# Attention of a two-layer decoder: its order worked out at build time, and small operations moved to GpSimd

## The chip, the cores and the metric

The kernel runs on one core of a Trainium2 chip. The metric is the device time of one execution in microseconds (us), here the median of three runs. A profiled execution gives a trace beside it: the time of every instruction, what each engine waited for, and TensorE's granted clock.

## The reference, cut to what matters

Two layers over 1024 positions of width 1024, all in float32. Layer A (a Mamba-2 scan) and the embedding steps aren't touched by the change. Layer B is stick-breaking attention with 16 heads of 64:

```python
kv = rmsnorm(h) @ w_kv                 # k normed per head, v
qg = rmsnorm(h) @ w_in                 # q normed per head, gate
for blk in range(8):                   # 128 queries at a time
    z = q[blk] @ k[:kend].T
    log_keep = where(strict, log_sigmoid(-z), 0)
    suffix = reverse_cumsum(log_keep) - log_keep
    weights = where(strict, exp(log_sigmoid(z) + suffix), 0)
    o[blk] = weights @ v[:kend]
out = (o * silu(gate)) @ w_out
```

Time runs backwards in the kernel, so that the suffix sums become running products of `sigmoid(-z)`, and the weights their differences. The kernel puts the difference on the values instead: `V` holds differences of neighbouring rows of v.

## The kernel before

Every float32 product is made of three matmuls: an operand is split into a high part and a low part (`hi`, `lo`), and hi x hi, hi x lo and lo x hi are summed (`split3`, `split3_some`, `terms`). The scores and the weights' products use two.

`attention` works through 8 pairs of heads (`hp`), and in each through four steps `p` = 3, 2, 1, 0 of 256 queries; 32 steps `i` in all. A step has these stages, which run in different steps at a time:

- `project` (two blocks `b` of 128 positions) and, twice a pair, `gate`: q, k, v and the gate from the weights `W[kk]` of the pair, 24 matmuls each. ScalarE copies the results to `kq` and `vr`.
- `values`: three loads on SP's queue shift `vr` by one row into `vs` (`nc.sync.dma_start(vs[0:P - 1], vr[1:P])` is the large one), two more spread its first row into `v0`; GpSimd subtracts and splits the result into `V`.
- `norm`: ScalarE squares `kq`, VectorE sums, takes the root (`Ctx.rstd`, `Ctx.rsqrt`: three small operations, then three turns of three) and multiplies `kq`.
- `flip`: TensorE transposes the normed keys and queries, ScalarE and VectorE split them into `kst`, `qh`, `ql`.
- `scores`: TensorE makes `z`, ScalarE the sigmoid into `pt`, VectorE the running product by one scan. Columns: 1024 - 128 b.
- `turn`, `product`, `fold`: TensorE transposes `pt`, ScalarE and VectorE split it into `wh` and `wl`, TensorE multiplies by `V` into `oqs`, the halves are added and gated into `GT`.

The weights of the next pair come by `Pairs.load`, one of four loads of 512 KB a step, split by `Ctx.hilo`: ScalarE makes the high part with the gain, VectorE the low part (line 110). They lie in a ring of 10 tiles and one of 2.

TensorE's order is written by hand: `step(i)` interleaves the projections of step i with the flip and scores of step i - 1 and the combination of step i - 2, at the fractions in `SPREAD` and `FLIP`. The other engines' orders are the scheduler's. After the last pair `b2.fill` runs part of the output projection for two blocks (7 and 6) ahead, from `s_out`, and `b2.pw.load` loads the last stage's gate weights inside the block with the hand-made order.

Of the kernel before, what the change touches and what calls it, by code (L numbers as in the profile page):

```python
# [18 lines left out]
P = 128  # L19
# [40 lines left out]
def terms(a, b):  # L60
    return [(a[0], b[0]), (a[0], b[1]), (a[1], b[0])]

# [723 lines left out]
def attention(k, A, rawp, hT, oTd, dbg, b2, pairs):  # L786
# [6 lines left out]
    with ExitStack() as ctx:  # L793
# [18 lines left out]
        def begin_pair(st):  # L812
            st["V"], st["vr"], st["v0"] = {}, {}, {}
            st["GT"] = pairs.gt.tile([P, S], F32, name="GT")

        def project(st, b):
            W = st["W"]
            ps = mm.tile([P, 512], F32, name="mm")
            prs = []
            sl = slice(b % 4 * P, b % 4 * P + P)  # L820
            for kk in range(KT):
                whi, wlo = W[kk]
                prs += terms((hh[b // 4][:, kk, sl], hl[b // 4][:, kk, sl]), (whi[:, :384], wlo[:, :384]))
            yield from split3_some(nc, ps[:, :384], prs, 2)
            p = b // 2
            if b % 2:
                st["kq"] = wk.tile([P, 2, 2, P], F32, name="kq", bufs=2)
                st["vr"][p] = wk.tile([P, 2, P], F32, name="vr", bufs=3)
            nc.scalar.copy(st["kq"][:, b % 2], ps.rearrange("p (m c) -> p m c", c=256)[:, :, 0:128])
            nc.scalar.copy(st["vr"][p][:, b % 2], ps[:, 128:256])  # L830
            yield

        def gate(st, half):
            W = st["W"]
            gp = mm.tile([P, 512], F32, name="mm")
            sl = slice(half * 512, half * 512 + 512)
            prs = []
            for kk in range(KT):
                whi, wlo = W[kk]
                prs += terms((whi[:, 384:], wlo[:, 384:]), (hh[half][:, kk], hl[half][:, kk]))  # L840
            yield from split3_some(nc, gp, prs, 2)
            sg = wk.tile([P, 512], F32, name="sg", bufs=1)
            nc.scalar.activation(sg, gp, AF.Sigmoid)
            nc.vector.tensor_tensor(st["GT"][:, sl], gp, sg, op=ALU.mult)
            yield

        def values(st, p):

            vr = st["vr"][p]
            vs = wk.tile([P, 2, P], F32, name="vs", bufs=1)  # L850
            nc.sync.dma_start(vs[0:P - 1], vr[1:P])
            nc.sync.dma_start(vs[P - 1:P, 0], vr[0:1, 1])
            nc.sync.dma_start(vs[P - 1:P, 1], st["vr"][p + 1][0:1, 0] if p < 3 else zrow)
            st["v0"][p] = sm.tile([P, 2], F32, name="v0", bufs=4)
            for i in range(2):
                nc.sync.dma_start(st["v0"][p][:, i:i + 1], vr[0:1, i])
            nc.gpsimd.tensor_tensor(vs, vs, vr, op=ALU.subtract)  # L857
            V = st["V"][p] = wk.tile([P, 2, 256], F32R, name="V", bufs=6)
            Vx = V.rearrange("p b (x c) -> p b x c", c=64)
            d = vs.rearrange("p b (h c) -> p b h c", c=64)  # L860
            for i in range(2):
                nc.gpsimd.tensor_copy(Vx[:, i, 0::3], d[:, i])
                nc.gpsimd.tensor_tensor(Vx[:, i, 1:3], d[:, i], Vx[:, i, 0::3].bitcast(F32), op=ALU.subtract)

        def norm(st, p):
            kq = st.pop("kq")
            sq = wk.tile([P, 512], F32, name="sg", bufs=1)
            nc.scalar.activation(sq, kq.rearrange("p b m c -> p (b m c)"), AF.Square)
            n = 8
            ss = sm.tile([P, n], F32, name="kss")  # L870
            nc.vector.reduce_sum(ss, sq.rearrange("p (g d) -> p g d", d=64), axis=AX.X)
            y = k.rstd(sm, ss, n, 64, EPS, "kr")
            x = kq.rearrange("p b m (h d) -> p (b m h) d", d=64)
            nc.vector.tensor_tensor(x, x, y.unsqueeze(2).broadcast_to([P, n, 64]), op=ALU.mult)
            st["kn", p] = kq

        def flip(st, p):
            kn = st.pop(("kn", p))
            tsl = slice(p * 256, (p + 1) * 256)
            kt, qt = (trp.tile([P, 512], F32, name="tr")[:, :256] for _ in range(2))  # L880
            for m, t in ((0, kt), (1, qt)):
                for i in range(2):
                    nc.tensor.transpose(t[:, i * P:(i + 1) * P], kn[:, i, m], ident)
            qh = wk.tile([P, 2, 256], F32R, name="qh", bufs=1)
            for h in range(2):
                o = own[h]
                nc.scalar.activation(kst[o, h, tsl], kt[o], AF.Copy, scale=k.gkq[o])
            for h in range(2):
                o, x = own[h], own[1 - h]
                nc.vector.scalar_tensor_tensor(  # L890
                    kst[x, h, tsl], kt[o], k.gkq[o], kst[o, h, tsl].bitcast(F32), op0=ALU.mult, op1=ALU.subtract)
            for h in range(2):
                o, x = own[h], own[1 - h]
                nc.scalar.copy(qh[o, h], qt[o])  # L894
                nc.scalar.copy(qh[x, h], qt[o])  # L895
            for h in range(2):
                o = own[h]
                nc.vector.tensor_tensor(ql[o, h], qt[o], qh[o, h].bitcast(F32), op=ALU.subtract)
            st["q", p] = qh

        def scores(st, h, b):

            N = (NT - b) * P
            qs = slice((b % 2) * P, (b % 2) * P + P)
            parts = [(0, N)] if N <= 512 else [(0, N // 2), (N // 2, N // 2)]
            def part(i):
                qh = st["q", b // 2]
                if i == 0:
                    st["a", h, b] = wk.tile([P, S], F32, name="pt", bufs=5)
                pt = st["a", h, b]  # L910
                ko, n = parts[i]
                z = zp.tile([P, 512], F32, name="z")
                rk = kst[:, h, b * P + ko:b * P + ko + n]
                nc.tensor.matmul(z[:, :n], lhsT=qh[:, h, qs], rhs=rk, start=True, stop=False)  # L914
                nc.tensor.matmul(z[:, :n], lhsT=ql[:, h, qs], rhs=rk, start=False, stop=True)  # L915
                nc.scalar.activation(pt[:, ko:ko + n], z[:, :n], AF.Sigmoid, scale=-1.0)  # L916
                if i == len(parts) - 1:
                    nc.vector.tensor_tensor_scan(pt[:, :N], pt[:, :N], keep[:, :N], 1.0, op0=ALU.mult, op1=ALU.max)  # L918
            return [lambda i=i: part(i) for i in range(len(parts))]

        def turn(st, p, h, j0):

            lo = 2 * p
            al, ah = st["a", h, lo], st["a", h, lo + 1]
            tq = trp.tile([P, 512], F32, name="tr")
            c = 0
            blocks = []
            for j in (j0, j0 + 1):
                i0 = (j - lo) * P
                nc.tensor.transpose(tq[:, c:c + P], al[:, i0:i0 + P], ident)  # L930
                w = P
                if j > lo:
                    nc.tensor.transpose(tq[:, c + P:c + 2 * P], ah[:, i0 - P:i0], ident)  # L933
                    w = 2 * P
                blocks.append((j, c, w))
                c += w
            wh = wk.tile([P, 512], F32R, name="wh", bufs=3)
            wl = wk.tile([P, 512], F32R, name="wl", bufs=3)
            nc.scalar.copy(wh[:, :c], tq[:, :c])  # L939
            nc.vector.tensor_tensor(wl[:, :c], tq[:, :c], wh[:, :c].bitcast(F32), op=ALU.subtract)  # L940
            blocks.sort(key=lambda x: -x[2])
            st["w", h, j0] = [(j, x[:, c:c + w], w) for x in (wh, wl) for j, c, w in blocks]

        def product(st, p, h, j0):
            out = oqs[:, h * 256:h * 256 + 256]
            ws = st.pop(("w", h, j0))
            for i, (j, rhs, w) in enumerate(ws):
                nc.tensor.matmul(out[:, :w], lhsT=st["V"][j // 2][:, j % 2, h * P:(h + 1) * P], rhs=rhs,  # L948
                                 start=(j0 == 2 * p and i == 0), stop=(j0 == NT - 2 and i == len(ws) - 1),
                                 skip_group_check=True)  # L950

        def fold(st, p, h):

            hp, GT, oq = st["hp"], st["GT"], oqs[:, h * 256:h * 256 + 256]
            if h == 0:
                st["of"] = wk.tile([P, 256], F32, name="of", bufs=2)
# [4 lines left out]
            if h == 0:  # L961
                return
# [328 lines left out]
```

## Time and profile before

| | us |
|---|---|
| median of 3 runs (1846.22 to 1849.69) | 1849.6 |
| the profiled execution's own time | 1852.96 |
| its span, first to last instruction | 1851.2 |
| TensorE busy in the span | 1731.0 |
| VectorE, ScalarE, GpSimd busy | 1173.9, 903.0, 413.2 |

Busy times are shares of one span and don't add up. A busy matmul is drawn from its start to its modelled end, and matmuls overlap, so the distance between starts says what one costs. The idle time before an instruction is put down to what released it last.

### The profile page before, as it was taken

The numbers are of one execution on the slowest core, as the hardware profiler recorded it, in microseconds if no ns is written. First come the engines' busy times: TensorE is split into PE (matmuls) and PEld (weight loads), VectorE is DVE, ScalarE is ACT, GpSimd is POOL, SyncE is SP. The second block draws the span as 40 slices with busy tenths as digits, with TensorE's granted clock in tenths as the row PEclk, the third lists the DMA queues.
The fourth block names the chain that finished last, engine by engine and source line by source line (L and its number), as shares of the span: only waits on it lengthen the run. The fifth ranks groups of instructions, "written<-read, shape, count | busy, mean of one in ns | idle before, by whom it ended". The sixth has DMA issues, their size and how long they took to land.

```text
span 1851.2 us, 25501 instructions
## 1 busy us (share of the span) xinstructions
PE 1731.0 (94%) x9170; PEld 1465.7 (79%) x9170; DVE 1173.9 (63%) x2396; ACT 903.0 (49%) x1976; POOL 413.2 (22%) x452
## 2 busy tenths in 40 slices
PE   7999999999999999999998989898989998689999
PEld 6777877877877887888887878787878888577887
DVE  6687277278179554335667786868787687674332
ACT  6567358349338332124546464655555555552211
POOL 0234534524634122200000111101101113211110
PEclk9999999999999999999998999999999999899999
DMA  4222223223213743322301010101011002224110
GB/s 154 66 81 92 80 66 91 95 58 93 90 62 98 248 158 124 123 94 78 106 19 62 20 53 19 52 31 39 32 46 57 19 29 73 73 86 127 43 44 34
DMA packets 96398, 139.43 MB, mean 75 GB/s; under 512 B 18160, under 2 KB 66640, under 8 KB 96272
## 3 DMA queue, kind: packets, MB, share of 16 engines
q1 hardware_dynamic: 96272, 137.80, 23.0%
q8 instruction: 72, 1.18, 0.3%
q14 instruction: 54, 0.44, 0.1%
HBM read 108.77 MB, written 24.77 MB: 72 GB/s over the span
## 4 chain that ended last, share of the span: by engine, by line
PE 74%; DVE 14%; ACT 7%; DMA 2%; issue 2%; POOL 1%; SPq 0%; DVEq 0%; POOLq 0%; ACTq 0%
PE mm L48 36%; PE mm L55 14%; PE mm L1122 5%; PE oq L948 3%; PE pq L48 2%; DVE pt L918 2%; PE z L915 2%; DVE v L236 2%; PE intra L411 2%; PE z L914 1%; PE tr L930 1%; PE inter L406 1%; ACT qh L895 1%; PE tr L666 1%; ACT qh L894 1%
## 5 line engine op out<-in xcount | busy, mean ns | idle before, releaser
L48 PE MATMUL mm<-ul,wh 128*128 128x512 f32 (+1 forms) x648 | 254.0, 392 | 0.0
L48 PE MATMUL mm<-uh,wl 128*128 128x512 f32 (+1 forms) x648 | 252.5, 390 | 0.0
L48 PE MATMUL mm<-uh,wh 128*128 128x512 f32 (+1 forms) x648 | 252.4, 389 | 0.1
L918 DVE TENSOR_TENSOR_SCAN pt<-pt,keep 128x128 f32<-128x128 f32 (+7 forms) x128 | 174.0, 1364 | 21.9 <-ACT pt L916 20.6
L55 PE MATMUL mm<-g0h,hl 128*128 128x384 f32 x512 | 182.5, 356 | 0.0
L55 PE MATMUL mm<-g0l,hh 128*128 128x384 f32 x512 | 182.3, 356 | 0.0
L55 PE MATMUL mm<-g0h,hh 128*128 128x384 f32 x512 | 181.1, 354 | 0.0
L236 DVE SCALAR_TENSOR_TENSOR v<-u,convh,v 128x512 f32<-128x512 f32 x144 | 130.2, 909 | 55.1 <-ACT v L234 52.7
L939 ACT CAST wh<-tr 128x512 fp32r<-128x512 f32 (+1 forms) x160 | 85.4, 543 | 146.6 <-PE tr L933 141.7
L857 POOL TENSOR_TENSOR vs<-vs,vr 128x256 f32<-128x256 f32 x32 | 24.1, 754 | 567.4 <-DMA vs<-vr 489.9
L940 DVE TENSOR_TENSOR wl<-tr,wh 128x512 fp32r<-128x512 f32 (+1 forms) x160 | 100.7, 633 | 72.6 <-ACT wh L939 71.8
L48 PEld LDWEIGHTS mm<-ul,wh 128*128 128x128 f32 x648 | 121.7, 188 | 26.4 <-issue 2.3
L48 PEld LDWEIGHTS mm<-uh,wl 128*128 128x128 f32 x648 | 121.8, 188 | 25.6 <-issue 1.9
L48 PEld LDWEIGHTS mm<-uh,wh 128*128 128x128 f32 x648 | 121.7, 188 | 25.6 <-issue 1.3
L108 POOL TENSOR_TENSOR wl<-raw,wh 128x1024 fp32r<-128x1024 f32 x39 | 95.2, 2441 | 156.7 <-ACT wh L106 156.7
L916 ACT ACTIVATE pt<-z 128x320 f32<-128x320 f32 (+3 forms) x192 | 93.8, 489 | 70.0 <-PE z L915 68.1
L55 PEld LDWEIGHTS mm<-g0l,hh 128*128 128x128 f32 x512 | 99.7, 195 | 2.1
L576 DVE SCALAR_TENSOR_TENSOR acc<-mm,rg,acc 128x512 f32<-128x512 f32 x64 | 47.8, 749 | 84.2 <-PE mm L48 83.3
L55 PEld LDWEIGHTS mm<-g0h,hl 128*128 128x128 f32 x512 | 99.7, 195 | 1.6
L55 PEld LDWEIGHTS mm<-g0h,hh 128*128 128x128 f32 x512 | 99.8, 195 | 1.2
L649 DVE SCALAR_TENSOR_TENSOR pth<-pth,pq 128x512 f32<-128x512 f32 (+1 forms) x33 | 22.2, 671 | 104.9 <-PE pq L48 100.2
L373 ACT ACTIVATE ex<-ex,acum 128x128 f32<-128x128 f32 x256 | 86.5, 389 | 0.8
(368 smaller groups left out, 4334.2 us busy)
## 6 DMA issues: line engine op xcount, KB each, us to landing
raw<-in_w_in SPq DMA_DIRECT2D x40, 512.0 KB
ex<-acd SPq DMA_DIRECT2D x64, 256.0 KB
raw<-in_w_b SPq DMA_DIRECT2D x32, 512.0 KB
raw<-in_m_out SPq DMA_DIRECT2D x16, 512.0 KB
raw<-in_gate SPq DMA_DIRECT2D x16, 512.0 KB
graw<-gT SPq DMA_DIRECT2D x30, 256.0 KB
gT<-zs SPq DMA_DIRECT2D x28, 256.0 KB
acc<-in_x SPq DMA_DIRECT2D x8, 512.0 KB
```

The lines of the kernel that those rows point to most:

```text
L48: nc.tensor.matmul(out, lhsT=a, rhs=b, start=(i == 0), stop=(i == n - 1))
L55: nc.tensor.matmul(out, lhsT=a, rhs=b, start=(i == 0), stop=(i == n - 1))
L108: (eng or nc.gpsimd).tensor_tensor(lo, raw, hi.bitcast(F32), op=ALU.subtract)
L236: nc.vector.scalar_tensor_tensor(vv, u[:, 3 - j:3 - j + 512], w(j), vv, op0=ALU.mult, op1=ALU.add)
L373: nc.scalar.activation(x, x, AF.Relu, bias=acum[:, c:c + 1])
L576: nc.vector.scalar_tensor_tensor(acc[:, sl], ps, k.rg[:, g, t:t + 1], acc[:, sl], op0=ALU.mult, op1=ALU.add)
L916: nc.scalar.activation(pt[:, ko:ko + n], z[:, :n], AF.Sigmoid, scale=-1.0)
L918: nc.vector.tensor_tensor_scan(pt[:, :N], pt[:, :N], keep[:, :N], 1.0, op0=ALU.mult, op1=ALU.max)
L939: nc.scalar.copy(wh[:, :c], tq[:, :c])
L940: nc.vector.tensor_tensor(wl[:, :c], tq[:, :c], wh[:, :c].bitcast(F32), op=ALU.subtract)
L948: nc.tensor.matmul(out[:, :w], lhsT=st["V"][j // 2][:, j % 2, h * P:(h + 1) * P], rhs=rhs, start=(j0 == 2 * p and i == 0), stop=(j0 == NT ...
L1122: nc.tensor.matmul(pss[n], lhsT=a, rhs=b, start=(q == 0 and i == 0), stop=(q == 1 and i == 11))
```

## The change

The attention is no longer emitted step by step. Each operation is entered into a `Plan` with its engine, a duration, a rank, what it comes after, and the buffers that it takes and gives back; `Plan.order` lists them, always taking the operation that can start first, at equal times the one with the lower rank. They are emitted in this order, and the order is now fixed on TensorE, ScalarE, VectorE and GpSimd (before: on TensorE alone). SP's loads are planned as three engines of their own (`SPV`, `SPW`, `SPS`).

The root's three turns go to GpSimd, as four operations each. The weights' gain is applied in place by ScalarE, which then copies the high part; the low part is a subtraction on GpSimd. Scans of over 512 columns are done in two parts. Sigmoid and product of the gate are made in `GT` itself. `b2.pw.load` stands behind the block. The core of the diff:

```diff
+class Plan:
+    LAT = 0.3
...
+    def order(self):
...
+            for i in open_:
+                eng, us, rank, _, after, takes, _ = self.ops[i]
+                t, ok, used = free.get(eng, 0.0), True, {}
+                for a in after:
+                    t = max(t, end[a] + (self.LAT if self.ops[a][0] != eng else 0.0))
...
+                        t = max(t, self.recs[taken[j]][2] + self.LAT)
+                if ok:
+                    key = (t, rank, i)
...
+        for name, bufs in (("mm", 2), ("z", 2), ("tr", 3), ("w", 3), ("pt", 5), ("kq", 2), ("vr", 3), ("qh", 1), ("sg", 1),
+                           ("of", 2), ("V", 6), ("vs", 1), ("raw", 3)):
...
+            rec, ids = chunks(10 * i + 5, 0.175, 2, make, prs, wdeps(hp))      # project
...
+            a = op_("ACT", 0.37, 10 * i + 1, copy_kq, ids[-1:], takes)
+            v = op_("ACT", 0.27, 10 * i + 1, lambda: nc.scalar.copy(sts[hp]["vr"][p][:, b % 2], tiles[key][:, 128:256]),
...
+            rec, ids = chunks(10 * i + 5, 0.232, 2, make, prs, wdeps(hp))      # gate
...
+        def values(i, hp, p, copies):
+            def load():
...
+                nc.sync.dma_start(vs[0:P - 1], vr[1:P])
+                nc.sync.dma_start(vs[P - 1:P, 0], vr[0:1, 1])
+                nc.sync.dma_start(vs[P - 1:P, 1], st["vr"][p + 1][0:1, 0] if p < 3 else zrow)
...
+            vd[i] = op_("SPV", 3.0, 10 * i, load, list(copies) + ([fgate[i - 4]] if i >= 4 else []), (vs_s,),
+            sub = op_("POOL", 0.74, 10 * i, lambda: nc.gpsimd.tensor_tensor(
...
+            vready[hp, p] = op_("POOL", 1.8, 10 * i, split, [sub], (V_s[i],), (vs_s,))
...
+            sq = op_("ACT", 0.63, 10 * i + 1, square, copies, (sg_s,))
...
+            rd = op_("DVE", 0.68, 10 * i + 1, sums, [sq], (), (sg_s,))
...
+            def turn_():
+                v, y, s = g["v"], g["y"], g["s"]
+                nc.gpsimd.tensor_tensor(s, y, v, op=ALU.mult)
+                nc.gpsimd.tensor_tensor(s, s, y, op=ALU.mult)
+                nc.gpsimd.tensor_scalar(s, s, -0.5, 1.5, op0=ALU.mult, op1=ALU.add)
+                nc.gpsimd.tensor_tensor(y, s, y, op=ALU.mult)
+            x = op_("DVE", 0.6, 10 * i + 1, start, [rd])
+            for _ in range(3):
+                x = op_("POOL", 1.0, 10 * i + 1, turn_, [x])
...
+            nmul[i] = op_("DVE", 0.69, 10 * i + 1, mul, [x])
...
+            fk = op_("PE", 0.22, 10 * i + 2, turn_(0), [nmul[i]], (ks,))
...
+                last = [z, op_("DVE", 0.15 + w * 0.00208, 10 * i + 3, scan, [s] + last[1:])]
...
+            rank = 40 * hp - 30 + 2 * q                                        # weights
...
+            ld = op_("SPW", 3.5, rank, load, [proj[hp - 1, 7 - 2 * q][0]], (r_s,))
...
+                        nc.scalar.activation(part(), part(), AF.Copy, scale=g)
+                        nc.scalar.copy(sts[hp]["W"][kk][0][:, sl], part())
...
+                        nc.gpsimd.tensor_tensor(lo[:, sl], part(), hi[:, sl].bitcast(F32), op=ALU.subtract)
+                    dep = [op_("ACT", 0.9, rank, high, [ld] + old + dep)]
+                    done.append(op_("POOL", 0.78, rank, low, dep, (), (r_s,)))
...
+            ld = op_("SPW", 4.0, rank - 20, load, extra + stored, (r_s,) + takes)   # fill
...
-        with tc.manual_schedule(engines={mybir.EngineType.PE}):
-            for i in range(n + 2):
-                step(i)
-            for _ in b2.pw.load(pairs.pool, 0):
-                pass
+        with tc.manual_schedule(engines={mybir.EngineType.PE, mybir.EngineType.Activation, mybir.EngineType.DVE, mybir.EngineType.Pool}):
+            for fn in plan.order():
+                fn()
+        for _ in b2.pw.load(pairs.pool, 0):
+            pass
```

## Rows read from the trace of the kernel before

**Rows 1.** The page, its parts 1 and 2: busy times, TensorE's busy tenths in slices.
```profile
PE 1731.0 (94%) x9170; PEld 1465.7 (79%) x9170; DVE 1173.9 (63%) x2396; ACT 903.0 (49%) x1976; POOL 413.2 (22%) x452
...
PE   7999999999999999999998989898989998689999
```

**Rows 2.** Windows: length, busy of PE, PEld, DVE, ACT, POOL; PEclk, DMA, GB/s.
```profile
1014.00:1100.00 86.00, 76.14 (x458) 70.00 (x457) 65.79 (x143) 47.55 (x115) 10.35 (x20) 0.98 0.12 38
...
1444.00:1530.00 86.00, 78.77 (x473) 72.74 (x472) 65.86 (x136) 46.93 (x112) 9.58 (x20) 0.98 0.08 25
...
1600.00:1662.00 62.00, 47.36 (x243) 38.63 (x243) 38.23 (x62) 27.34 (x55) 13.32 (x9) 0.85 0.31 97
```

**Rows 3.** SP's queue by time: start, us, line, operation.
```profile
1041.50 0.64 SPq L851 DMA_DIRECT2D vs<-vr  x1
...
1074.95 0.34 SPq L760 DMA_DIRECT2D raw<-in_w_b  x1
...
1469.17 0.64 SPq L851 DMA_DIRECT2D vs<-vr  x1
```

**Rows 4.** The chain that ended last, by time: start, us, what.
```profile
934.45 2.79 PE mm L55 x16
...
1571.40 1.39 PE mm L55 x6
...
1590.73 0.41 PE oq L948 x4
...
1592.89 0.47 PE oq L948 x4
...
1648.42 0.22 PE tr L930 x2
```

**Rows 5.** Waits of TensorE from 920 to 1660: us in total, times, longest.
```profile
PE oq L948 <- DVE wl L940: 19.9, 14, 1.8
PE z L915 <- DVE ql L898: 17.5, 15, 1.6
...
PE tr L883 <- DVE kq L874: 8.6, 6, 3.9
...
PE mm L1122 <- POOL V L108: 7.5, 1, 7.5
```

**Rows 6.** Windows of 20 us, the one before a change of pairs.
```profile
1080.00:1100.00 20.00, 15.36 (x96) 13.51 (x95) 17.35 (x39) 11.19 (x27) 3.52 (x5) 1.00 0.25 82
```

**Rows 7.** Groups by line and shape: busy us, mean ns; idle before.
```profile
L918 DVE TENSOR_TENSOR_SCAN pt<-pt,keep 128x128 f32<-128x128 f32 (+7 forms) x128 | 174.0, 1364 | 21.9 <-ACT pt L916 20.6
L918 DVE TENSOR_TENSOR_SCAN pt<-pt,keep 128x1024 f32<-128x1024 f32 x16 | 36.6, 2287 | 0.8
L110 DVE SCALAR_TENSOR_TENSOR g0l<-raw,kvn,g0h 128x256 fp32r<-128x256 f32 x54 | 26.3, 486 | 1.0 <-PE z L915 0.9
L80 DVE SCALAR_TENSOR_TENSOR krs<-krs,kry 128x8 f32<-128x8 f32 x96 | 16.4, 171 | 2.7
L108 POOL TENSOR_TENSOR pl<-praw,ph 128x256 fp32r<-128x256 f32 x16 | 12.2, 762 | 201.0 <-ACT ph L106 200.9
L233 POOL COPY u<-u 128x3 f32<-128x3 f32 x24 | 4.9, 204 | 60.1 <-issue 41.7 <-ACT u L229 14.5 <-DVE v L236 3.9
```

**Rows 8.** ScalarE by time.
```profile
1041.19 0.29 ACT L830 COPY vr<-mm 128x128 f32<-128x128 f32 x1
...
1081.82 0.51 ACT L106 ACTIVATE g0h<-raw,kvn 128x256 fp32r<-128x256 f32 x1 [1.80 <-DMA raw<-in_w_b]
```

**Rows 9.** GpSimd by time.
```profile
1049.65 0.73 POOL L857 TENSOR_TENSOR vs<-vs,vr 128x256 f32<-128x256 f32 x1 [20.09 <-DMA vs<-vr]
...
1050.94 0.87 POOL L863 TENSOR_TENSOR V<-vs,V 128x128 fp32r<-128x128 f32 x2
...
1082.12 2.09 POOL L863 TENSOR_TENSOR V<-vs,V 128x128 fp32r<-128x128 f32 x2
```

**Rows 10.** VectorE by time.
```profile
1082.22 1.74 DVE L918 TENSOR_TENSOR_SCAN pt<-pt,keep 128x640 f32<-128x640 f32 x1
```

More of the change, by code (lines that the diff above doesn't have):

```diff
@@ L833, in gate @@
[L833 to L836, printed above, removed]
+        plan = Plan()
+        for name, bufs in (("mm", 2), ("z", 2), ("tr", 3), ("w", 3), ("pt", 5), ("kq", 2), ("vr", 3), ("qh", 1), ("sg", 1),
+                           ("of", 2), ("V", 6), ("vs", 1), ("raw", 3)):
+            plan.ring(name, bufs)
+        op_, slot = plan.op, plan.slot
+        sts = pairs.sts
+        sts[0].update(V={}, vr={}, v0={})
@@ new lines, in attention, with chunks, go @@
+        tiles = {}
+        proj, gmul, wready, vready = {}, {}, {}, {}
+        nmul, kq_s, vr_s, V_s, vd = {}, {}, {}, {}, {}
+        khi, klo, qlo, zs, scans, pt_s = {}, {}, {}, {}, {}, {}
+        fadd, fgate, last_turn, last_prod, rows_done = {}, {}, {}, {}, {}
+        mm_last = []
+        steps = [(hp, p) for hp in range(8) for p in range(NT // 2 - 1, -1, -1)]
+        n = len(steps)
+        def chunks(rank, us, m, make, prs, after_of, first=()):
+            rec, ids = slot("mm"), []
+            for c in range(0, len(prs), m):
+                def go(c=c):
+                    if c == 0:
+                        make()
+                    for i in range(c, min(c + m, len(prs))):
+                        a, b, out = prs[i]()
+                        nc.tensor.matmul(out, lhsT=a, rhs=b, start=(i == 0), stop=(i == len(prs) - 1))
+                after = list(after_of(c, min(c + m, len(prs)) - 1))
+                after += ids[-1:] if c else list(first) + mm_last[-1:]
+                ids.append(op_("PE", us * m, rank, go, after, (rec,) if c == 0 else ()))
+            mm_last.append(ids[-1])
+            return rec, ids
@@ L837, in gate, with wdeps, deps, project @@
+        def wdeps(hp):
+            def deps(c0, c1):
+                return [x for kk in {c0 // 3, c1 // 3} for x in wready.get((hp, kk), ())]
+            return deps
+        def project(i, hp, b):
+            p = b // 2
+            key = ("ps", hp, b)
+            def make():
+                tiles[key] = mm.tile([P, 512], F32, name="mm")
+            sl = slice(b % 4 * P, b % 4 * P + P)
             prs = []
             for kk in range(KT):
-                whi, wlo = W[kk]
-                prs += terms((whi[:, 384:], wlo[:, 384:]), (hh[half][:, kk], hl[half][:, kk]))
@@ L841, in gate @@
[L841 to L875, printed above, removed]
@@ L877, in flip, with pr @@
-        def flip(st, p):
-            kn = st.pop(("kn", p))
-            tsl = slice(p * 256, (p + 1) * 256)
[L880 to L884, printed above, removed]
+                for t in range(3):
+                    def pr(kk=kk, t=t):
+                        w = sts[hp]["W"][kk]
+                        x, y = terms((hh[b // 4][:, kk, sl], hl[b // 4][:, kk, sl]), (w[0][:, :384], w[1][:, :384]))[t]
+                        return x, y, tiles[key][:, :384]
+                    prs.append(pr)
@@ L892, in flip @@
[L892 to L901, printed above, removed]
+                prev = [op_("ACT", 0.73, 10 * i + 2, query_hi(h), [fq] + prev, (qh_s,) if h == 0 else ())]
+                pd = [op_("DVE", 0.43, 10 * i + 2, query_lo(h), prev + pd + old, (), (qs,))]
@@ L903, in scores, with parts @@
+                qlo[i, h] = pd[0]
+            return qh_s
+        def parts(b):
+            N = (NT - b) * P
+            return [(0, N)] if N <= 512 else [(0, N // 2), (N // 2, N // 2)]
+        def scores(i, hp, h, b, qh_s):
             N = (NT - b) * P
             qs = slice((b % 2) * P, (b % 2) * P + P)
[L905 to L918, printed above, removed]
@@ L944, in product @@
[L944 to L956, printed above, removed]
-            t = st["of"]
-            o, x = own[h], own[1 - h]
-            nc.scalar.copy(t[o], oq[x, :256])
-            nc.vector.tensor_tensor(t[o], oq[o, :256], t[o], op=ALU.add)
-            if h == 0:
-                return
-            for i in range(2):
-                g = GT[:, p * 256 + i * P:p * 256 + (i + 1) * P]
-                nc.vector.scalar_tensor_tensor(
-                    g, t[:, i * P:(i + 1) * P], st["v0"][p][:, i:i + 1], g, op0=ALU.add, op1=ALU.mult)
+            pt_s[i, h, b] = slot("pt")
@@ new lines, in s_out, with load, high, low @@
+        def s_out(kk):
+            rank = 305 + 2 * kk
+            half, j = 1 - kk // 4, kk % 4
+            r_s = slot("raw")
+            old = [x[-1] for key, x in proj.items() if key[0] == 7 and (
+                (key[1] // 4 == half) if key[1] != "g" else key[2] == half)]
+            def load():
+                tiles["raw", 8, kk] = rawp.tile([P, 1024], F32, name="raw")
+                nc.sync.dma_start(tiles["raw", 8, kk], A["s_out"][kk * P:(kk + 1) * P, :])
+            ld = op_("SPW", 3.5, rank, load, [proj[7, 5][0]], (r_s,))
+            sl = slice(2 * j, 2 * j + 2)
+            v = lambda: tiles["raw", 8, kk].rearrange("p (n c) -> p n c", n=2)
+            def high():
+                if j == 0:
+                    b2.big = [b2.hp.tile([P, KT, 512], F32R, name=f"{x}{half}") for x in ("hh", "hl")]
+                tiles["big", half] = b2.big
+                b2.W[kk] = [tuple(x[:, 2 * j + m] for x in b2.big) for m in range(2)]
+                nc.scalar.copy(b2.big[0][:, sl], v())
+            first = sdone.get(kk - 1, ())
+            a = op_("ACT", 1.06, rank, high, [ld] + old + list(first)[:1])
+            eng, us = ("DVE", 1.25) if kk in (5, 7) else ("POOL", 2.4)
+            def low():
+                hi, lo = tiles["big", half]
+                (nc.vector if eng == "DVE" else nc.gpsimd).tensor_tensor(lo[:, sl], v(), hi[:, sl].bitcast(F32), op=ALU.subtract)
+            sdone[kk] = (a, op_(eng, us, rank, low, [a], (), (r_s,)))
@@ new lines, in attention @@
+        for hp in range(8):
+            pair = [(4 * hp + 3 - p, p) for p in (3, 2, 1, 0)]
+            for i, p in pair:
+                copies = project(i, hp, 2 * p + 1)
+                if p == 1:
+                    gate(i, hp, 1)
+                    gate(i, hp, 0)
+                copies += project(i, hp, 2 * p)
+                norm(i, hp, p, (copies[0], copies[2]))
+                values(i, hp, p, (copies[1], copies[3]))
+            if hp + 1 < 8:
+                for q in range(4):
+                    weights(hp + 1, q)
+            if hp == 6:
+                begun.append(op_("SPW", 0.0, 0, lambda: b2.begin(pairs), proj[6, 0][-1:]))
+            for i, p in pair:
+                qh_s = flip(i, hp, p)
+                for h in range(2):
+                    for b in (2 * p + 1, 2 * p):
+                        scores(i, hp, h, b, qh_s)
+                combine(i, hp, p)
```

457 lines of the change are left out of this document (333 added, 124 removed).

## The prediction

> **What bounds the kernel now.** I read the busy times first: TensorE is busy for 1731.0 of 1851.2 us, every other engine far less [rows 1]. That share looks like a kernel with nothing left, so the next question is where its idle time lies. The slices show full tenths up to attention and a change of 8 and 9 in it [rows 1], and the windows give the amount: TensorE is busy for 76.1 of 86 us in the first of six such stretches of attention and for 78.8 in the last [rows 2]. Attention repeats itself: the load of the second step's values starts at 1041.50 in one pair of heads and at 1469.17 five pairs later, so a pair takes 427.67 / 5 = 85.5 us [rows 3].
>
> How much of that is TensorE's own work comes from the spacing of matmuls on the chain of waits [rows 4]. Per pair of heads: 8 projections of 24 at 2.79 / 16 = 0.174 us make 33.5; two gates of 24 at 1.39 / 6 = 0.232 make 11.1; 2 x 9216 score columns at 1.39 / (6 x 512) us make 8.3; 72 transposes at 0.22 / 2 = 0.11 make 7.9; products of 12 wide and 8 narrow units at 0.47 and 0.41 make 8.9; 16 transposes of keys and queries make 1.8. The sum is 71.5 us. So 85.5 - 71.5 = 14 us of each pair are TensorE idle, at the lower of its two clocks (the granted clock is 0.98 of 2.4 GHz over the stretch, so a part of it ran at 1.2; in the tail, where TensorE stands for 15 of 62 us, it is 0.85 [rows 2]) or busy only in name, with a matmul's end drawn out before a wait. With eight pairs that is 112 us, all that a better order can win in attention.
>
> The waits say who is late [rows 5]: `wl` (the low parts of the attention weights, made by VectorE) for 19.9 us, `ql` for 17.5, the normed keys for 8.6. They lie around the change of pairs, where VectorE is busy for 17.4 of 20 us and TensorE for 15.4 [rows 6]. There the low parts of the next pair's projection weights, the root and the longest scans come together on VectorE.
>
> **The change part by part.**
>
> *Off VectorE.* 16 low parts a pair at 26.3 / 54 = 0.49 us are 7.8 us, and 4 x 9 small operations of the root at 0.171 are 6.2 [rows 7]. Scans cut in two add a fixed part: 2.287 us at 1024 columns and 1.364 at the mean of 576 leave 0.18 at none [rows 7], times 8 a pair is 1.4. VectorE falls from 65.8 [rows 2] to 65.8 - 7.8 - 6.2 + 1.4 = 53 us.
>
> *Onto ScalarE.* The gain is now applied in place and the high part copied, one operation more for each half tile. Such a copy isn't in attention; a gain operation of the same size takes 0.51 [rows 8], and nothing of that size can be free, so 16 of them cost 6 to 8 us; I take 8. ScalarE goes from 47.6 to 56 us.
>
> *Onto GpSimd.* 16 subtractions of 256 columns at 0.762 are 12.2 us. The root's tensor operations of 8 columns are not in the trace on this engine: a copy of 3 columns takes 0.204 [rows 7], and 0.762 scaled down to 8 columns is 0.02, so the 4 x 12 of a pair lie between 1 and 10 us; they are nearest to the copy, and I take 10. GpSimd goes from 10.3 to 33 us. All three stay below 71.5, so none of them becomes the bound by its sum.
>
> *The order.* The plan starts each operation as soon as its inputs are ready, so an operation has no time in hand beyond the 0.3 us of latency that is added at each change of engine. Its durations agree with the rows: 0.175 for a projection matmul, 0.232 for a gate's, 0.74 and 0.78 on GpSimd. One doesn't. It counts 3.0 us for the load of `vs`. The trace has the load issued at 1041.50, right behind the copy of `vr` (1041.19 + 0.29), and GpSimd's subtraction starts at 1049.65 [rows 3, 8, 9]: 8.15 us. Before, nobody minded: only the values' own operations sat behind it on GpSimd. After the change the root's turns and the weights' low parts do.
>
> I follow one step through the plan, from the copy of its queries and keys. The values' subtraction is ready after 0.3 + 0.3 + 3.0 + 0.3 = 3.9 us, the first turn of the root after square, sums, start and three latencies, some 2.8 to 4. The subtraction and the split behind it have the lower rank, so at least the last turn, mostly two or three, are put behind them. In truth the subtraction starts at 0.3 + 8.15 = 8.4. The turns behind it are late by up to 4.5; against that stand four hops that the plan counts at 0.3 each (the issue of the load came 0.02 us behind its copy [rows 3, 8]; I take 0.15 a hop as too much), and up to 1 us that the subtraction would have waited for a turn. So the normed keys come 2.9 to 3.9 us after their place in TensorE's order; I take 3.25. The transposes of those keys stand in a fixed order, and projections, scores and products of the other steps are queued behind them on TensorE.
>
> How often is this paid? Not four times a pair. While TensorE stands for step p = 3, the load of p = 2 has been running: its projection (24 x 2 matmuls, 8.4 us) is the filler between p = 3's copy and its transposes. The gates (11.1 us) then separate p = 2 from p = 1, and p = 0 follows p = 1 as p = 2 follows p = 3. So I count two stalls, 6.5 us a pair.
>
> *The change of pairs.* There are 10 + 2 buffers for eight weight tiles a pair, so some six tiles wait for the last projection that reads the old ones. Each needs 2 x (0.51 + 0.51) = 2 us of ScalarE, 12 us in all, against what TensorE has then: of step p = 1, with 1408 of 4608 columns, 0.31 x (8.3 + 7.9 + 8.9) = 7.7 us, and the first scores of p = 0. I take 3 us of idle time; below nothing it can't go, above it would be 8 if GpSimd's low parts also sat behind a values' load.
>
> *The weights' load* is planned at 3.5 us. One issued at 1074.95 was waited for by ScalarE until 1081.82 [rows 3, 8], 6.9 us. Three buffers hold it over most of the previous pair, so I cost it at nothing; uncovered it holds ScalarE's queue, sigmoids behind it, for 3.4 us a pair.
>
> *The tail.* TensorE waits 7.5 us there for one operand of the output projection [rows 5], in a stretch with 47 of 62 us busy [rows 2]. The plan may pull these up (12 us at most), but its loads are again too short (4.0 us), and the gate weights of the last stage are now written behind the planned block, ten tiles, each at most twice the 0.49 of a half tile (10 us if nothing covers them). I take the two as even: 0, between -12 and +10.
>
> *Sum.* A pair takes 71.5 + 3 (change of pairs) + 6.5 (two stalls) + 1 (clock, about what the stalls of before cost) = 82 us instead of 85.5. Eight pairs give 28 us. The profiled execution took 1852.96 us around a span of 1851.2, 3.4 above the median of 1849.6; with 28 off it would be 1825, and the median 1849.6 - 28 = 1821.6.
>
> **The rivals.**
>
> *The plan holds.* The late load is covered: norms wait long enough for VectorE that the values are there first. For it: VectorE's long scans stand before the norm in rank. Then a pair takes 71.5 + 3 + 1 = 75.5, and the time is 1849.6 - 80 = 1770.
>
> *GpSimd's queue, every step.* The stall is paid at all four steps, because the steps' projections lie too far apart to share it, or because the low parts of the next pair's weights are caught behind p = 0's load. For it: one queue now serves three users, and the 8.15 us stand in it at every step. Against it: VectorE's backlog, which holds the norms back as well. Then 71.5 + 3 + 4 x 3.25 + 1 = 88.5 a pair, +24 us: 1874. It turns to the slower side at three stalls (85.3).
>
> *The shared interface.* Two subtractions of 128 columns on GpSimd took 2.09 us where the scan of 1.74 us ran beside them, and 0.87 without one [rows 9, 10]: they seem to stand still in a scan. With 174 / 8 = 22 us of scans in a pair [rows 7], the root's 3 us and the split's 1.5 are stretched by a third: two stalls longer by 1.5 make 85 a pair, 4 us less in all: 1846. The Trainium skill (GPSIMD Engine Reference, Key points) says that GpSimd shares its SBUF interfaces with VectorE and meets contention when VectorE has two SBUF inputs, and that VectorE does elementwise work twice as fast; by that rule the moved work is worth little and 1846 would be the time. The trace agrees with the contention in that row.
>
> **How the numbers follow.** Chances: two stalls 0.38 (1806 to 1838), the plan holds 0.27 (1750 to 1800), every step 0.25 (1850 to 1890), the interface 0.10. The likeliest gives 1822. The range, 1762 to 1870, leaves out the lower part of the second case and the upper of the third, some 0.2. A change within 0.2% (3.7 us) can't be told from none here. Faster: 0.38 + 0.27 and a third of the last, 0.68. Same: half of the last and the three-stall edge of the third, 0.08. Slower: 0.24.
>
> **What would show it.** The distance between loads of `vs` a pair apart should be 82 us. TensorE's waits should be led by the transposes of the keys, waiting for VectorE's product `kq`, once or twice a pair for about 3 us, with GpSimd's subtraction waiting for the load of `vs` in front of the turns; `wl` and `ql` should have fallen off the list. If no such wait is there, the plan holds; if four, the second rival; if GpSimd's turns are several times 0.2 us, the third. The prediction is wrong altogether if the tail gives or takes more than 12 us.

## The result and the profile after

The changed kernel takes 1870.1 us (median of 4 runs, 1869.87 to 1871.41) against 1849.3 for the kernel before, measured beside it: 1.0118 of its time, with a 95% interval of 1.01 to 1.0135. It is slower by 21 us; 28 less had been forecast.

First the page of the changed kernel, its parts 1 and 2: busy times, and the tenths of TensorE and of its granted clock.

```profile
span 1869.7 us, 25848 instructions
...
PE 1745.8 (93%) x9170; PEld 1478.1 (79%) x9170; DVE 1123.4 (60%) x2060; ACT 944.5 (51%) x2088; POOL 618.6 (33%) x948
...
PE   7999999999999999999988989898998899689999
...
PEclk9999999999999999999998989898999999799999
```

VectorE lost 50 us against [rows 1], GpSimd gained 205, and TensorE is busy for 15 us more with the same 9170 instructions. The span is 18.5 us longer. From the first matmul of attention's projections to the last it is 677.0 us (925.9 to 1602.9) where it was 667.3, so 9.7 more; from there to the end 266.8 instead of 256.8, so 10.0 more.

The windows of the changed kernel, columns as in [rows 2]: one pair of heads, another pair, and the tail.

```profile
1014.00:1101.90 87.90, 75.96 (x444) 69.59 (x444) 57.77 (x97) 52.86 (x128) 38.03 (x87) 0.95 0.12 37
1277.60:1365.40 87.80, 81.20 (x468) 75.81 (x468) 62.02 (x100) 54.77 (x132) 38.98 (x86) 0.92 0.12 37
1610.00:1676.00 66.00, 50.97 (x234) 41.04 (x235) 57.39 (x91) 39.34 (x81) 21.67 (x25) 0.83 0.38 113
```

The granted clock lies between 0.92 and 0.95 in all five such stretches (mean 0.936); before, it was 0.96 to 0.98 (mean 0.973 of six). The tail stands as long as in [rows 2] and at a similar clock. The moved work is all there: VectorE is busy for 58 to 62 of 88 us (53 had been forecast), ScalarE for 53 to 55 (56), GpSimd for 38 to 39 (33); none is near to being the bound.

SP's queue in the changed kernel, the load of one step's values, five pairs apart as in [rows 3]:

```profile
1033.02 0.64 SPq L982 DMA_DIRECT2D vs<-vr  x1
...
1472.66 0.66 SPq L982 DMA_DIRECT2D vs<-vr  x1
```

A pair takes 439.64 / 5 = 87.9 us where it took 85.5 and where 82 was forecast. TensorE's waits over the whole run (us in total, times, longest) name what is late:

```profile
PE tr L1049 <- DVE kq L1038: 45.5, 14, 9.6
PE mm L905 <- POOL g0l L1244: 19.9, 23, 2.8
...
PE z L1106 <- DVE ql L1076: 6.7, 11, 0.8
...
PE oq L1164 <- DVE wl L1156: 1.7, 4, 1.0
```

The waits that led the list before, `wl` and `ql` [rows 5], fell from 37.4 us to 8.4. The transposes of the normed keys took their place: 35.9 us in 13 waits in attention, and one of 9.6 in the tail. Behind them come the low parts of the weights, now made on GpSimd. Here is one such wait on three engines. First SP and GpSimd of the changed kernel by time; the bracket is the idle time before an instruction:

```profile
1000.80 0.67 SPq L982 DMA_DIRECT2D vs<-vr  x1
```

```profile
1003.37 0.20 POOL L1031 TENSOR_TENSOR kry<-krs,kry 128x8 f32<-128x8 f32 x1
1009.79 0.74 POOL L991 TENSOR_TENSOR vs<-vs,vr 128x256 f32<-128x256 f32 x1 [6.22 <-issue]
...
1011.73 0.45 POOL L1001 TENSOR_TENSOR V<-vs,V 128x128 fp32r<-128x128 f32 x1
1012.14 0.20 POOL L1028 TENSOR_TENSOR krs<-kry,krv 128x8 f32<-128x8 f32 x1
...
1014.11 0.20 POOL L1031 TENSOR_TENSOR kry<-krs,kry 128x8 f32<-128x8 f32 x1
```

Then VectorE and TensorE:

```profile
1014.35 1.20 DVE L1038 TENSOR_TENSOR kq<-kq,kry 128x512 f32<-128x512 f32 x1 [5.12 <-POOL kry L1031]
```

```profile
1015.60 1.11 PE L1049 MATMUL tr<-ident,kq 128*128 128x128 f32 x4 [4.67 <-DVE kq L1038]
```

The load is issued at 1000.80. GpSimd has done one turn of the root (the last of its four operations at 1003.37), reaches the subtraction of the values, stands for 6.22 us until 1009.79, splits the values, and only then does the other two turns. `kq` needs the last of them, and TensorE stands for 4.67 us. For these 6.22 us the profile names no releaser (`issue`); that it is the load, 8.99 us after its issue, is read from the like stands whose row names it (`vs<-vr`, 93.4 us in all, shown further down). What follows on TensorE, in windows of 4 us of the changed kernel:

```profile
1006.00:1010.00 4.00, 3.81 (x23) 3.51 (x22) 2.55 (x4) 3.25 (x9) 0.21 (x1) 1.00 0.06 20
1010.00:1014.00 4.00, 0.93 (x6) 0.66 (x5) 0.00 (x0) 0.87 (x2) 3.29 (x12) 1.00 0.00 0
1014.00:1018.00 4.00, 2.40 (x9) 2.41 (x10) 3.55 (x3) 1.06 (x3) 3.38 (x5) 0.63 0.02 0
1018.00:1022.00 4.00, 4.00 (x24) 3.97 (x24) 3.86 (x6) 3.43 (x10) 0.00 (x0) 0.94 0.43 136
1022.00:1026.00 4.00, 4.00 (x29) 3.85 (x28) 3.73 (x10) 3.64 (x9) 0.00 (x0) 1.00 0.08 24
```

After a stretch with 0.93 of 4 us busy, the granted clock averages 0.63 over the next 4 us, so most of them run at 1.2 GHz (1.00 is 2.4), and it is back at 0.94 and 1.00 in the windows after. The matmuls from 1017.15 to 1018.11 start 0.32 us apart, those from 1019.32 on 0.17 to 0.18. This stall is paid for twice, once as idle time and once as slower matmuls that look busy.

The same shows over the whole of attention, from its first projection to its last. The windows of the kernel before, of the changed kernel, and of the changed kernel with one number of its plan put right (the first experiment below):

```profile
927.00:1594.40 667.40, 600.72 (x3529) 554.18 (x3528) 504.38 (x1090) 366.19 (x873) 87.94 (x161) 0.96 0.12 39
926.00:1603.00 677.00, 609.34 (x3510) 562.25 (x3508) 447.22 (x756) 403.75 (x974) 282.63 (x625) 0.94 0.13 40
927.00:1533.00 606.00, 573.07 (x3515) 534.56 (x3513) 432.73 (x758) 404.32 (x978) 306.62 (x640) 0.99 0.14 44
```

TensorE is idle for 66.7, 67.7 and 32.9 us. The changed kernel stands no longer than the one before; what grew is the busy time, by 8.6 us for nearly the same matmuls, with the granted clock at 0.94 instead of 0.96. Against the third row, 35 us more of idle time come with 36 us more of busy time. But not every wait is paid for twice: the 33 us that the third row still has, the longest wait 2.4 us, go with a clock of 0.99.

### The profile page after: what moved, and what is told of

The parts are those of the page before. It is cut to its first block, busy times and chain, and to the rows that moved or that the text cites. A ratio compares the mean times of both kernels' runs of the same rounds, so it can differ in the third digit from the quotient of the medians.

```text
span 1869.7 us, 25848 instructions
## 1 busy us (share of the span) xinstructions
PE 1745.8 (93%) x9170; PEld 1478.1 (79%) x9170; DVE 1123.4 (60%) x2060; ACT 944.5 (51%) x2088; POOL 618.6 (33%) x948
## 5 line engine op out<-in xcount | busy, mean ns | idle before, releaser
L905 PE MATMUL mm<-g0l,hh 128*128 128x384 f32 x512 | 186.7, 365 | 20.2 <-POOL g0l L1244 19.9
L1118 DVE TENSOR_TENSOR_SCAN pt<-pt,keep 128x320 f32<-128x320 f32 (+3 forms) x192 | 198.8, 1055 | 10.4 <-ACT pt L1113 5.8
L1156 DVE TENSOR_TENSOR wl<-tr,wh 128x512 fp32r<-128x512 f32 (+1 forms) x160 | 96.1, 632 | 18.9 <-ACT wh L1151 17.2
L1113 ACT ACTIVATE pt<-z 128x320 f32<-128x320 f32 (+3 forms) x192 | 89.5, 493 | 29.9 <-PE z L1106 26.6
L1244 POOL TENSOR_TENSOR g0l<-raw,g0h 128x256 fp32r<-128x256 f32 x112 | 94.5, 874 | 30.5 <-ACT g0h L1240 30.3
L905 PEld LDWEIGHTS mm<-g0h,hh 128*128 128x128 f32 x512 | 103.6, 202 | 0.9
L905 PEld LDWEIGHTS mm<-g0h,hl 128*128 128x128 f32 x512 | 103.7, 203 | 0.7
L711 ACT ACTIVATE pth<-mm,prh 128x512 f32<-128x512 f32 (+1 forms) x33 | 22.3, 675 | 129.7 <-PE mm L48 128.9
```

Source lines behind the costliest of these rows:

```text
L711: nc.scalar.activation(th, g, AF.Tanh, scale=rh)
L905: nc.tensor.matmul(out, lhsT=a, rhs=b, start=(i == 0), stop=(i == len(prs) - 1))
L1113: nc.scalar.activation(tiles[key][:, ko:ko + w], tiles["z", i, h, b, m][:, :w], AF.Sigmoid, scale=-1.0)
L1118: nc.vector.tensor_tensor_scan(pt[:, ko:ko + w], pt[:, ko:ko + w], keep[:, ko:ko + w], pt[:, ko - 1:ko] if ko else 1.0, op0=ALU.mult, op1= ...
L1156: nc.vector.tensor_tensor(wl[:, :c], tiles["tq", key][:, :c], wh[:, :c].bitcast(F32), op=ALU.subtract)
L1244: nc.gpsimd.tensor_tensor(lo[:, sl], part(), hi[:, sl].bitcast(F32), op=ALU.subtract)
```

## The experiments

The theory after the result: the plan's short duration, 3.0 us for a load that takes 8 to 9, puts the values' subtraction in front of the root and of the weights' low parts on GpSimd, and everything lost comes from that. The rivals: GpSimd is too slow for the moved work, by its own durations or by the interface that it shares; or the new order is bad by itself; or the weights' load, planned too short as well, costs. Times are medians in us; ratios, with their 95% intervals, are to the kernel before on the same chip, whose medians are 1849.4 to 1849.6.

**The plan is told the truth: 3.0 becomes 8.2.**

```diff
-            vd[i] = op_("SPV", 3.0, 10 * i, load, ...
+            vd[i] = op_("SPV", 8.2, 10 * i, load, ...
```

> The load of the values is planned with 8.2 us instead of 3.0; no other edit, so the same operations stand in another order. Late load (my theory): the waits of TensorE's key transposes for kq (45 us in all) are gone, the granted clock rises from 0.93 to 0.96 or more, and the time is 1800 to 1830. Rival, the fixed greedy order itself is slow: the waits move to other places and the time stays at 1855 to 1875. Rival, shared interface: GpSimd's work is as stretched as before, 1855 to 1870.

Measured: 1790.3 us, 0.9679 [0.9663, 0.9696], 10 better than the best expected. One number in the plan is worth 80 us. Every transfer and operation is the same; only the order differs, on all four engines. TensorE's waits in attention and tail of this kernel, SP's queue as above, and a window in the middle of attention:

```profile
PE oq L1164 <- DVE wl L1156: 10.8, 8, 1.7
PE z L1106 <- DVE ql L1076: 7.8, 9, 1.6
PE tr L1049 <- DVE kq L1038: 7.5, 6, 1.9
...
PE mm L905 <- POOL g0l L1244: 2.6, 9, 0.6
```

```profile
1027.08 0.65 SPq L982 DMA_DIRECT2D vs<-vr  x1
...
1412.73 0.65 SPq L982 DMA_DIRECT2D vs<-vr  x1
```

```profile
1014.00:1100.00 86.00, 81.26 (x502) 75.71 (x501) 64.37 (x106) 59.31 (x146) 46.96 (x93) 1.00 0.14 45
```

A pair takes 385.65 / 5 = 77.1 us. The keys' waits fell from 45.5 us to 7.5, the low parts' from 19.9 to 2.6, and the clock is 1.00 in this window (0.99 over attention).

**The load is made short, and the plan keeps 3.0.** The transfer of 127 rows is cut in two:

```diff
-                nc.sync.dma_start(vs[0:P - 1], vr[1:P])
+                nc.sync.dma_start(vs[0:112], vr[1:113])
+                nc.sync.dma_start(vs[112:P - 1], vr[113:P])
```

> The plan is left as it is (3.0 us); the large load of 127 rows is cut into 112 and 15 rows, two transfers. By the rule of the Trainium skill on how many DMA engines a transfer uses, 112 rows go over 16 engines and 127 over one. Late load: if the load is shorter (3 to 4 us from issue to the subtraction), the plan's number comes true and the time is 1800 to 1830, without any change of order. If the load stays at 8 us: 1868 to 1875, and nothing is learnt of the theory. Rival, the fixed greedy order: a shorter load leaves 1855 to 1870.

Measured: 1807.0, 0.9769 [0.9748, 0.9791]. In this kernel the load issued at 1083.72 is used 4.1 us later:

```profile
1083.72 0.54 SPq L982 DMA_DIRECT2D vs<-vr  x1
```

```profile
1087.80 0.73 POOL L992 TENSOR_TENSOR vs<-vs,vr 128x256 f32<-128x256 f32 x1 [4.54 <-DMA vs<-vr]
```

GpSimd's idle time now names the load. The keys' waits are as many as before the cut and shorter (14.2 us in 14, the longest 2.8). The plan and its order are those of the changed kernel. So the lateness itself costs, and a shorter transfer cures 63 of the 80 us without a word to the plan. The Trainium skill (DMA: Bandwidth & Descriptors, "Why a DMA increments its semaphore by 16 and not by 1") says that a transfer is spread over the largest number of engines, up to 16, that divides its slowest dimension: one for 127 rows, and so 16 for 112. The times agree, 8 to 9 us for the one piece and 4.1 for the two. So does the share of the 16 DMA engines that is busy: 0.06, one sixteenth, in the changed kernel's window from 1006 to 1010 above, where the one piece runs alone; and in this kernel 0.36 and then 0.10 in the two us from 1058.90, behind a load issued at 1057.90 with no other large one beside it.

**Short load and true plan together** (the two pieces, planned at 4.2):

> The load in two pieces (4.1 us from issue to subtraction in the run before) and planned with 4.2 us. Late load: the plan is true and the load short, so this is at least as fast as either alone: 1775 to 1792. Rival, what is left in e1 has nothing to do with the load: 1788 to 1793, as with the 8 us load rightly planned.

Measured: 1797.4, 0.9715 [0.9697, 0.9732], slower than both expectations and no better than the slow load told truly. Once the plan knew the duration, the transfer's length was worth nothing here. Why this order comes out 7 us behind the first experiment's stays open.

**The kernel before with the short load**, the same two lines in it:

> The kernel before with the load in two pieces. Late load: in the kernel before nothing but the values' own operations stands behind the load, and they have some ten us in hand, so 1845 to 1852, no change. Rival, the shorter load by itself was the gain of e2: 1800 to 1830.

Measured: median 1862.0 of ten, ratio 1.0052 [1.0022, 1.0083], a miss: 1845 to 1852 had been expected. The ten scatter from 1844.2 to 1868.5; why they do stays open. A shorter load gained nothing here, so the gain of the cut load in the changed kernel is not the short transfer by itself. That fits the reading of [rows 9], that the values' own operations alone stood behind the load.

**Root back on VectorE, load at 3.0.** Three operations a turn, entered as such:

```diff
-                x = op_("POOL", 1.0, 10 * i + 1, turn_, [x])
+                x = op_("DVE", 0.6, 10 * i + 1, turn_, [x])
```

> The root's turns go back to VectorE (three operations each, planned at 0.6 us a turn), planned load of 3.0 us kept. Late load: the root no longer stands behind the subtraction on GpSimd, so the waits for kq fall to a third or less; the low parts of the weights still stand there. 1825 to 1850. Rival, fixed greedy order: 1860 to 1875. Rival, VectorE is the bound around the change of pairs and needs the root away: slower than 1870.

Measured: 1796.8, 0.9717 [0.9702, 0.9731], 28 us better than the best expected. The wrong load stays and costs little: the root is no longer behind it (the keys' waits are 13.6 us in 9, of which one of 6.9), and the low parts, which still are, hold TensorE for 7.5 us in 11 waits.

**Low parts back on VectorE, load at 3.0.**

```diff
-                    dep = [op_("ACT", 0.9, rank, high, [ld] + old + dep)]
-                    done.append(op_("POOL", 0.78, rank, low, dep, (), (r_s,)))
+                    dep = [op_("ACT", 0.5, rank, high, [ld] + old + dep)]
+                    done.append(op_("DVE", 0.49, rank, low, dep, (), (r_s,)))
```

> The low parts of the weights go back to VectorE in their old form (one ScalarE operation less for each), root and planned load as in the changed kernel. Late load: the root still stands behind the subtraction, so the waits for kq stay near 45 us; the 20 us of waits for the low parts go. 1845 to 1862. Rival, the low parts on GpSimd and the second ScalarE operation are what costs: 1830 or less.

Measured: 1829.2, 0.9887 [0.9872, 0.9902]: a miss, 41 us better than the changed kernel where 8 to 25 had been allowed, and inside the band of the rival that the low parts themselves are what costs. That rival doesn't hold by itself: the first experiment keeps them on GpSimd and takes 1790.3, and with the true plan their place makes no difference (below). TensorE's first wait in this kernel shows that the keys' stalls stayed as they were:

```profile
PE tr L1049 <- DVE kq L1038: 44.1, 13, 8.0
```

What went are the 19.9 us of waits for `g0l`, and the granted clock from 1000 to 1500 us rose from 0.94 to 0.97; that difference over the 677 us of attention is some 20 us. Other waits grew a little (`wl` from 1.7 to 10.0), so all of TensorE's waits together fell by some 17; with the clock that is 37 of the 41. I had left the clock out of the expectation. That waits and clock go down together fits here, but wasn't isolated.

**The root in front of the subtraction, load at 3.0.** The subtraction is made to come after the last turn of its step; no other edit is made, though the plan may then order other operations differently too:

```diff
+            rooted[i] = x
...
-                ... subtract), [vd[i]], (), (vr_s[i],))
+                ... subtract), [vd[i], rooted[i]], (), (vr_s[i],))
```

> The load is still planned with 3.0 us and takes 8; the one edit is that the values' subtraction comes after the root's three turns of the same step in GpSimd's order. Late load, with the root queued behind it as the harm: the waits for kq (45 us) are gone and the time is 1795 to 1825; what is left behind the load are the low parts. Rival, the load is harmful because the values themselves come late to TensorE's products: the waits for kq go but waits of the products for V take their place, 1850 or more.

Measured: 1788.3, 0.9671 [0.9655, 0.9687], 7 better than the best expected. The load is as slow and planned as wrongly as in the changed kernel, and 82 us are gone. SP's and GpSimd's rows of this kernel:

```profile
1007.13 0.63 SPq L982 DMA_DIRECT2D vs<-vr  x1
```

```profile
1014.89 1.04 POOL L1031 TENSOR_TENSOR kry<-krs,kry 128x8 f32<-128x8 f32 x1
1015.89 0.74 POOL L991 TENSOR_TENSOR vs<-vs,vr 128x256 f32<-128x256 f32 x1
```

The subtraction starts 8.76 us after the issue of its load, with no idle time: the root has run inside the load's time. TensorE's waits for `kq` are 1.5 us in one; the low parts, still behind the load, hold it for 9.2 us in 16. This pins the cause to a place in GpSimd's queue and not to the number 3.0 as such.

**What the moved work is worth with the true plan.** Load at 8.2, low parts back on VectorE:

> Load planned with 8.2 us, low parts of the weights back on VectorE, root on GpSimd. Late load, with the low parts on GpSimd worth something of their own: 1800 to 1815, slower than e1's 1790 because VectorE gets 7.8 us a pair back. Rival, low parts on GpSimd cost as much as they give (shared interface, second ScalarE operation): 1775 to 1790.

Measured: 1790.6, 0.9686 [0.9671, 0.97], at the edge of the rival by which the low parts cost on GpSimd as much as they give. Load at 8.2, root back on VectorE, low parts on GpSimd:

> Load planned with 8.2 us, root back on VectorE, low parts on GpSimd. The fourth corner beside e1 (both on GpSimd, 1790), f2 (root alone, 1791) and f3 (neither, 1796). If each move is worth little once the plan is true: 1788 to 1798. If the root on GpSimd is the move that counts: 1795 to 1800.

Measured: 1800.3, 0.9732 [0.9718, 0.9747], nearer to the case in which the root's move counts. Load at 8.2 and both back, so that only the order and its details (scans in two parts, the gate in `GT`, `b2.pw.load` behind the block) are new:

> Load planned with 8.2 us, root and low parts both back on VectorE: the planned order on four engines alone. If the order is what gives: 1790 to 1815. If the moves to GpSimd give it (VectorE's backlog at the change of pairs): 1835 to 1850, near the kernel before.

Measured: 1796.2, 0.9715 [0.9701, 0.973]. All corners but one, in us:

| on GpSimd | load planned 8.2 | load planned 3.0 |
|---|---|---|
| root and low parts | 1790.3 | 1870.1 |
| root only | 1790.6 | 1829.2 |
| low parts only | 1800.3 | 1796.8 |
| neither | 1796.2 | not run |

The order with its details gives 53 us. In the column of 8.2 the root on GpSimd gives 6 to 10 more, the low parts nothing or a loss of 4; orders that differ in planned durations alone scatter as much (below), so neither is shown. In the column of 3.0 the harm doesn't add up: behind the late load the low parts alone cost nothing (1796.8 against 1800.3), the root alone 39 us (1829.2 against 1790.6), both together 80. Why the low parts cost 41 only where the root stands there too stays open.

**The weights' load, planned at 3.5 and 4.0**, raised to 7.0 and 8.0 on top of the 8.2, first alone:

> As e1 (values' load planned with 8.2 us), and the other loads planned with what they take as well: the weights' 7.0 instead of 3.5, the output projection's 7.0, the last two blocks' 8.0 instead of 4.0. If the short weights' load costs something in e1: 1778 to 1787. If three buffers hide it, as the prediction had it: 1788 to 1793.

Measured: 1791.3, 0.9687 [0.9672, 0.9701], the same as without: that load is hidden. Then with the low parts back on VectorE:

> As the one before, with the low parts of the weights back on VectorE. If the low parts on GpSimd cost as much as they give, as f2 against e1 showed: the same as the one before within 4 us.

Measured: 1781.1, 0.9622 [0.9601, 0.9643], the best version, 68 us below the kernel before and 89 below the changed one. A miss on the good side: 10 us less than the run above it, while the same move was worth nothing at 3.5. In this kernel five pairs lie 381.6 us apart, 76.3 each, and TensorE's waits in attention and tail are led by

```profile
PE tr L1049 <- DVE kq L1038: 9.7, 7, 3.3
PE oq L1164 <- DVE of L1184: 6.1, 2, 4.0
PE oq L1164 <- DVE wl L1156: 4.8, 4, 2.3
```

So orders that differ only in the planned durations of loads can lie 10 us apart (this run and 1790.6); which of the plan's choices makes them wasn't tried.

## Why the prediction was wrong

**The place was right.** The late load of the values, GpSimd's queue behind it, root and low parts in that queue, TensorE at the transposes of the keys: each was forecast, and each is in the rows and in the runs that take one link away (load told truly, load shortened, root moved off, root put first).

**Stalls at the keys: sized a little too high.** Forecast two of 3.25 us a pair, 6.5. Measured 13 of 2.76 us in eight pairs, 4.5 a pair. The rival with a stall at every step ended nearest to the time, 1874, but not by its count: it wanted 32 stalls. Of its two reasons the second, low parts caught behind a load, is what the rows show. That the time lies next to the upper end of the range, which that rival set, is luck.

**The change of pairs: the size was right, its cause was not.** The prediction let 3 us stand for it, for ScalarE's splitting of the weights, with 8 as the upper end "if GpSimd's low parts also sat behind a values' load". TensorE's list has no wait for ScalarE's high parts. It has the low parts: 19.9 us, 2.5 a pair.

**The clock was the term that failed.** Forecast 1 us a pair, "about what the stalls of before cost". The mean granted clock of 0.936 costs up to 0.064 x 87.9 = 5.6 us a pair (less by as much as TensorE stood in it), against 2.3 at the 0.973 of before. So the term was short even for the stalls of before, and it let the clock rise although waits were forecast to remain. They remained in full: idle time in attention is 67.7 us against 66.7. And the 14 us that I wanted to win contained such a part, and some 3 us that neither waits nor clock explain. The pair by measured terms: 71.5 + 4.5 (keys) + 2.5 (low parts) + 0.8 (`ql`) + up to 5.6 (clock) = 84.9, and some 3.0 left over, against 87.9; I had 71.5 + 3 + 6.5 + 1 = 82. What speaks for the 71.5 is the first experiment: there the clock is 1.00 from 1014 to 1530, the waits listed come to some 32 us up to the last projection and 42 with the tail, 4.0 to 5.3 a pair, and 71.5 + 4.0 to 5.3 = 75.5 to 76.8 against 77.1.

**The tail was 0 only with the load told truly.** Forecast 0 between -12 and +10; measured +10.0, at the edge. 9.6 us of it are one wait for `kq`, the same fault on a last step:

```profile
1604.32 0.73 POOL L991 TENSOR_TENSOR vs<-vs,vr 128x256 f32<-128x256 f32 x1 [9.25 <-DMA vs<-vr]
```

```profile
1612.86 1.12 PE L1049 MATMUL tr<-ident,kq 128*128 128x128 f32 x4 [9.62 <-DVE kq L1038]
```

With the load at 8.2, the stretch from the last projection to the end is 256.7 us, that of before 256.8.

**The sum.** Eight pairs at +2.4 would be 19, but attention measured +9.7. The five pairs between the two loads took 12.0 us more, the stretch ahead of the first of these loads (from the first projection) 7.3 less, the one behind the second (to the last projection) 5.0 more. The tail adds 10.0 and the stretch ahead of attention takes 1.2 off: the span's 18.5. Against the forecast of 28 less that is 46.5 us, of which attention has 37.7 and the tail 10.0.

**The rivals.** "The plan holds" (75.5 a pair, 1770) describes the kernel with one number changed: 77.1 and 1790. The shared interface is seen and doesn't decide. The groups of the changed kernel on GpSimd and ScalarE, columns: busy, mean ns, idle before:

```profile
L1244 POOL TENSOR_TENSOR g0l<-raw,g0h 128x256 fp32r<-128x256 f32 x112 | 94.5, 874 | 30.5 <-ACT g0h L1240 30.3
...
L1030 POOL TENSOR_SCALAR krs<-krs 128x8 f32<-128x8 f32 x96 | 28.0, 292 | 8.4
L991 POOL TENSOR_TENSOR vs<-vs,vr 128x256 f32<-128x256 f32 x32 | 27.9, 873 | 174.2 <-DMA vs<-vr 93.4 <-ACT pt L1113 19.2 <-ACT wh L1151 18.0
```

```profile
L1240 ACT CAST g0h<-raw 128x256 fp32r<-128x256 f32 x112 | 45.5, 406 | 3.5
```

The low part takes 0.874 us where 0.762 stood in [rows 7], the root's operations 0.24 to 0.29 in the mean of a line where 0.20 is their usual row. VectorE is stretched too: the product `kq` takes 0.98 in the mean where it took 0.71, and the scans are busy for 198.8 us instead of 174.0, 3.1 a pair where 1.4 had been forecast; this is part of why VectorE fell less than the prediction had it. Yet the first experiment carries all this work with a like stretch (0.916 for the low part, 0.911 for `kq`) and takes 1790 us. What that rival said of the moved work, that it is worth little, holds: at the true plan it is 10 us at most. The largest row is the third: 93.4 us in which GpSimd stands in front of a subtraction because of the load. The copy on ScalarE costs 0.41, 6.5 us a pair, within the 6 to 8 forecast.

## What to carry to other kernels

When an order is fixed at build time and each engine takes its operations in it, as here, an instruction that waits for a DMA is a gate for all that stands behind it: measure each load from issue to first use and plan with that, and put nothing urgent behind it that does not need it. Price long waits on TensorE up to twice, as the wait and as the lower clock after it, and expect both back as long as such waits remain; short ones cost less (33 us of them went with a clock of 0.99 here). Try the new order before moving work to another engine: here the order gave 53 us, the root's move 6 to 10 more, and the low parts' move between nothing and 10 less, and moves of that size can't be told from the scatter of the orders.

## What the hardware showed that was not expected

- A transfer of 127 rows of 1 KB inside SBUF takes 8 to 9 us from issue to use, with a sixteenth of the DMA engines' time busy; cut in 112 and 15 rows it takes 4.1.
- A stand of 4.67 us up to 1015.60 goes with a mean granted clock of 0.63 from 1014 to 1018. Over attention the changed kernel has 35 us more idle time than the one with the true plan, and 36 us more busy time for nearly the same matmuls.
- GpSimd's operations of 128x8 take 0.20 us undisturbed, 0.28 from start to start (1012.14, 1012.42, 1012.71, 1012.99), and up to 1.07 beside VectorE's scans (the run with the root first, 1012.11).
